# Hybrid decoder layer on one core: seven block products in place of eight in the up-projection, and a down projection of its own

## The chip, the cores and the metric

The kernel runs on one core of one Trainium2 chip. The metric is the time of one execution on the device in microseconds. Engines are named as in the profile: PE is TensorE (PEld its weight loads), DVE is VectorE, ACT is ScalarE, POOL is GpSimd, SP is SyncE, which only issues transfers.

## The reference, cut to what matters

One decoder layer, 512 positions, width 2048, everything in float32. Three groups of attention heads are mixed and projected back; then comes the feed-forward part, which the change concerns. D_FF is 5632, so `w_up` is 2048 x 11264.

```
x = x + einsum('bse,ed->bsd', mix, w_out[l])
h = rmsnorm(x, ffn_norm[l])
u = causal_dwconv(einsum('bsd,df->bsf', h, w_up[l]), conv_w[l], conv_b[l])   # three taps along the sequence
gate, up = split(u, [D_FF], axis=-1)
x = x + einsum('bsf,fd->bsd', silu(gate) * up, w_down[l])
```

## The kernel before, in words

Activations lie transposed: 16 row tiles of 128 features x 512 positions. To keep float32 accuracy at the fast rate of the float32r type, each operand is split in two float32r parts, hi (a conversion on ScalarE) and lo (the remainder, a subtraction on VectorE), and each product of a 128 x 128 weight block with a 128 x 512 activation tile is made of three matmuls, hi hi, hi lo and lo hi (`mm3`, line 262). All projections go through `product` (line 290): it takes one of two PSUM banks `pj`, accumulates over the row tiles, and spawns a task that uses the result.

Weights come in a fixed `stream` of pieces of 128 x 1024 (0.5 MB): `load_next` (line 234) issues a load into one of three buffers `wr`, `split_next` (line 241) converts half a piece at a time into buffers `wh` and `wl`, four of each, three halves ahead of their use.

The order of work is written by the program itself: the kernel is emitted in the order of a simulated clock (`Clock`, line 80) that advances with TensorE's modelled time. Small tasks are generators that yield until the clock passes their last instruction; `clock.run` resumes those that are due, `idle` moves the clock on, `drain` empties the queue. Within an engine the emitted order is the executed order; between engines semaphores are placed by the framework.

The output projection has two halves. `project_ab` (line 882) multiplies the eight tiles of groups A and B while the last heads of group C still run, and adds to the residual tiles `xn` in SBUF. Then 16 products over the tiles of group C follow, and the task `projected(m)` (line 935) scales each by the group's norm (`rg`), adds it to `xn[m]`, splits the result times the norm's gain into hi and lo (`xg2`, 32 tiles), and sums the squares on GpSimd (`sumsq`, `row_rstd`), whose result `r2` scales the rows of the up-projection afterwards.

The feed-forward part runs in chunks of eight feature tiles of the 44 (the last chunk has four). One feature tile needs two products over 16 row tiles, gate and up, so 96 matmuls of 512 columns; `conv` (line 964) applies norm, bias and taps, `gate` and `up` make silu(gate) * up and split it. The down products of one chunk, 16 of them over the chunk's tiles, are interleaved with the up-projection of the next chunk, and `summed` (line 1003) adds each to `xn[m]`.

```
        for op in ffn:
            if op[0] == "up":
                f = op[1]
                product(xg2, conv(f, f, gate))
                product(xg2, conv(NFF + f, f, up))
            else:
                c0, n = chunks[op[1]]
                product([("g", f) for f in range(c0, c0 + n)], summed(op[1], op[2]))
```

Below stand the functions that the diff touches and what calls them.

## Time and profile before

| what | value |
|---|---|
| median of 3 runs | 2230.79 us (2230.22 to 2231.01) |
| the profiled execution | 2230.37 us, its span 2228.6 us |
| TensorE busy, share of the span | 2217.2 us, 99% |
| VectorE, ScalarE, GpSimd busy | 54%, 44%, 5% |
| bytes moved | 244.26 MB, 110 GB/s in the mean |

The span runs from the first to the last instruction of the program; the execution's time has 1.8 us more around it. A busy TensorE is not TensorE at its peak, since the ends of matmuls are modelled: what a stream of them costs is read from the distance of their starts. A group of instructions is named by line, engine, operation and what it writes and reads (out<-in); line 50 is the helper through which the compute instructions are issued.

### The profile page before, as it was taken

What the parts mean: (1) busy time and instruction counts of PE and PEld (TensorE: products, weight loads), DVE (VectorE), ACT (ScalarE), POOL (GpSimd) and SP (SyncE); (2) the same over time, 40 slices, a digit from 0 to 9 for tenths busy, and PEclk for the clock granted to TensorE, in tenths of its full rate; (3) what the DMA queues carried; (4) which work ended last, traced back from release to release, by engine and by line L of the source; (5) the groups of instructions that cost most, each with busy time, mean ns of one, the idle gap of its engine ahead of it and who ended that gap; (6) DMA issues with size and microseconds to landing.
All of it is one profiled execution on the core that took longest, in us unless ns stands there. A gap on an engine that the chain in (4) does not pass through costs nothing.

```text
span 2228.6 us, 27035 instructions
## 1 busy us (share of the span) xinstructions
PE 2217.2 (99%) x10068; PEld 1838.5 (82%) x10068; DVE 1211.9 (54%) x2091; ACT 983.8 (44%) x1864; POOL 100.7 (5%) x153
## 2 busy tenths in 40 slices
PE   8999999999999999999999999999999999999999
PEld 6888888888888888888888888888888888888887
DVE  7676777767755655444444444444444444443444
ACT  6778667776754443333233333333333333232322
POOL 4000100110100200000000000000000000000000
PEclk9999999999999999999999999999999999999999
DMA  6333343334644333233333333333233333333324
GB/s 199 96 95 97 109 146 117 114 107 151 216 136 145 95 99 100 95 95 97 102 95 95 97 103 95 95 96 103 95 95 95 103 96 95 95 101 97 95 86 141
DMA packets 83082, 244.26 MB, mean 110 GB/s; under 512 B 9784, under 2 KB 13240, under 8 KB 82952
## 3 DMA queue, kind: packets, MB, share of 16 engines
q1 hardware_dynamic: 82952, 242.55, 35.0%
q8 instruction: 79, 1.29, 0.2%
q14 instruction: 51, 0.42, 0.1%
HBM read 223.05 MB, written 12.64 MB: 106 GB/s over the span
## 4 chain that ended last, share of the span: by engine, by line
PE 98%; DMA 1%; DVE 0%; issue 0%; SPq 0%; ACT 0%; DVEq 0%; ACTq 0%
PE pj L50 91%; PE s L50 5%; PE po L50 2%; PE c L50 1%; DMA wr<-in_w_in_dram 0%; DVE wl L50 0%; DMA st<-in_xT_dram 0%; SPq L128 0%; DVE sq L50 0%; DVE x L50 0%; ACT x L50 0%; DVE o L50 0%; DVE pt L50 0%; DVE sc L50 0%; ACT wh L50 0%
## 5 line engine op out<-in xcount | busy, mean ns | idle before, releaser
L50 ACT CAST wh<-wr 128x512 fp32r<-128x512 f32 (+2 forms) x782 | 476.1, 610 | 1075.4 <-PE pj L50 993.6
L50 PE MATMUL pj<-xg,wh 128*128 128x512 f32 x2816 | 867.3, 389 | 0.0
L50 DVE TENSOR_TENSOR wl<-wr,wh 128x512 fp32r<-128x512 f32 (+2 forms) x782 | 539.8, 692 | 511.5 <-ACT wh L50 503.8
L50 PE MATMUL pj<-x,wh 128*128 128x512 f32 x2272 | 710.2, 394 | 0.0
L50 PEld LDWEIGHTS pj<-xg,wh 128*128 128x128 f32 x2816 | 528.5, 188 | 110.3 <-issue 0.5
L50 PE MATMUL pj<-xg,wl 128*128 128x512 f32 x1408 | 547.7, 389 | 0.0
L50 PEld LDWEIGHTS pj<-x,wh 128*128 128x128 f32 x2272 | 415.3, 188 | 80.9 <-issue 3.0
L50 PE MATMUL pj<-x,wl 128*128 128x512 f32 x1136 | 443.7, 391 | 0.0
L50 PEld LDWEIGHTS pj<-xg,wl 128*128 128x128 f32 x1408 | 264.3, 188 | 54.8
L50 PE MATMUL pj<-mc,wh 128*128 128x512 f32 x896 | 275.7, 389 | 0.0
L50 PEld LDWEIGHTS pj<-x,wl 128*128 128x128 f32 x1136 | 213.2, 188 | 46.0
L50 PEld LDWEIGHTS pj<-mc,wh 128*128 128x128 f32 x896 | 168.2, 188 | 35.0
L50 PE MATMUL pj<-mc,wl 128*128 128x512 f32 x448 | 174.3, 389 | 0.0
L50 DVE TENSOR_TENSOR x<-pj,x 128x512 f32<-128x512 f32 x112 | 77.4, 691 | 130.3 <-PE pj L50 130.3
L50 DVE SCALAR_TENSOR_TENSOR cv<-sq,conv,cv 128x511 f32<-128x511 f32 (+1 forms) x176 | 132.2, 751 | 28.0 <-ACT cv L50 24.9
L50 DVE TENSOR_TENSOR sq<-pj,r 128x512 f32<-128x512 f32 x88 | 60.9, 692 | 138.8 <-PE pj L50 138.7
L50 PEld LDWEIGHTS pj<-mc,wl 128*128 128x128 f32 x448 | 84.1, 188 | 17.4
L50 DVE CUSTOM_DVE_ANT_0 sc<-s,strip 128x128 f32<-128x128 f32 (+3 forms) x96 | 43.7, 455 | 75.6 <-PE s L50 75.2
L50 ACT ACTIVATE cv<-sq,conv 128x512 f32<-128x512 f32 x88 | 71.9, 817 | 28.3 <-DVE sq L50 28.3
L50 ACT ACTIVATE sc<-sc,nm 128x128 f32<-128x128 f32 (+2 forms) x96 | 50.2, 526 | 1.4 <-DVE nm L50 1.3
L50 ACT CAST pt<-s 128x128 fp32r<-128x128 f32 (+2 forms) x96 | 35.7, 398 | 26.9 <-PE s L50 26.3
L50 ACT ACTIVATE sc<-sc,dn 128x128 f32<-128x128 f32 (+2 forms) x96 | 43.5, 525 | 4.3 <-DVE dn L50 4.2
(115 smaller groups left out, 1316.7 us busy)
## 6 DMA issues: line engine op xcount, KB each, us to landing
wr<-in_w_up_dram SPq DMA_DIRECT2D x176, 512.0 KB, 3.4
wr<-in_w_down_dram SPq DMA_DIRECT2D x80, 512.0 KB, 3.4
wr<-in_w_in_dram SPq DMA_DIRECT2D x78, 512.0 KB, 3.5
wr<-in_w_out_dram SPq DMA_DIRECT2D x32, 512.0 KB, 3.5
st<-st SPq DMA_DIRECT2D x48, 128.0 KB, 4.3
strip<-rb SPq DMA_DIRECT2D x24, 256.0 KB, 3.8
st<-in_xT_dram SPq DMA_DIRECT2D x16, 256.0 KB, 4.0
o_dram<-o SPq DMA_DIRECT2D x16, 256.0 KB, 4.4
```

The costliest lines, as they stand in the source:

```text
L50: res = issue(out, *args, **kwargs)
```

## The change

The up-projection is seen as a product of 2 x 2 blocks and takes seven block products instead of eight (Winograd's form of Strassen's scheme). The weights are cut into gate and up columns, and into even and odd row tiles; the activations into even and odd row tiles, and into the two halves of the sequence, 256 positions each (`HS`).

- For each pair of row tiles, `forms` makes seven blocks of 128 x 256 from the gained residual: three of the four blocks themselves and four sums, split in `TH` and `TL`, 8 tiles each, kept for the whole stage.
- For each of the 44 feature tiles (u), seven steps take a weight operand of 128 x 1024: three are blocks of `w_up` (a11, a12, a22), two are sums that the transfer makes, a plain load followed by an accumulating one issued from GpSimd (p, v), and two are sums made on VectorE (q, r). `cast` and `rest` split them three steps ahead. A step is 8 x 3 matmuls of 256 columns; four partial sums stand in halves of two PSUM banks and are copied out between steps on ScalarE. The up rows come out negated, so `nr2` is the negative of `r2`.
- `after` also does the norm, the convolution, the SiLU and the product of the tile before, and stores the result g to `g_dram`.
- Before the stage the clock is drained. The residual is kept in DRAM: `project_ab` stores it to `xab_dram`, `projected` reads it there and stores the sum to `xm_dram`.
- The down projection follows as a stage of its own: all 44 tiles g are loaded back and split (`gates`); six output tiles are accumulated chunk by chunk in six PSUM banks, the other ten one after the other over all 44 tiles. The matmuls are those of before in number and shape.

```diff
-        for op in ffn:
-            if op[0] == "up":
-                stream += [w_up[2 * t + i] for t in (op[1], NFF + op[1]) for i in range(2)]
-            else:
-                stream.append(w_down[op[1]][op[2]][:, :chunks[op[1]][1] * 128])
...
                 def task(pt):
                     vector.tensor_add(xn[m], pt, xn[m])
                     give(pt)
-                    return
-                    yield
+                    yield
+                    load(xab_dram[m], xn[m])
...
+            while "rg" not in ready or any(("mix", i) not in ready for i in MIX_ORDER[8:]):
+                idle()
+            clock.run()
+        xctx.close()
+        tctx = ctx.enter_context(ExitStack())
+        tp = tctx.enter_context(tc.tile_pool(name="tp", bufs=1, side="right", reuse_waits="tile"))
+        tr = tctx.enter_context(tc.tile_pool(name="tr", bufs=1, side="right", reuse_waits="tile"))
+        TH = [tp.tile([128, 7 * HS], F32R, name=f"th{j}") for j in range(8)]
+        TL = [tp.tile([128, 7 * HS], F32R, name=f"tl{j}") for j in range(8)]
...
+        def reload_x(m):
+            t = tr.tile([128, S], F32, name="xn", bufs=3)
+            load(t, xab_dram[m])
+            xs2.append(t)
+        def forms(j):
+            a, b = xb[2 * j], xb[2 * j + 1]
+            f = tr.tile([128, 4 * HS], F32, name="sm", bufs=2)
+            q = [f[:, i * HS:(i + 1) * HS] for i in range(4)]
+            vector.tensor_sub(q[0], a[:, :HS], a[:, HS:])
+            scalar.copy(TH[j][:, :HS], a[:, :HS])
+            vector.tensor_sub(q[1], b[:, HS:], a[:, HS:])
+            scalar.copy(TH[j][:, HS:3 * HS], b)
+            vector.scalar_tensor_tensor(q[2], b[:, HS:], -1.0, q[0], op0=ALU.mult, op1=ALU.subtract)
+            vector.scalar_tensor_tensor(q[3], q[2], -1.0, b[:, :HS], op0=ALU.mult, op1=ALU.subtract)
             yield
-            ready["mix", m] = scaled_split(t, sm[:, SM_MG + m:SM_MG + m + 1], *pair(fp, "mc", 16))
-        for i in MIX_ORDER[8:]:
-            spawn(mix_split(i))
-        spawn(group_rstd())
-        while m < KT:
-            project_ab(m)
-            m += 1
-        xg2 = [("y", m) for m in range(KT)]
-        acc = []
+            scalar.copy(TH[j][:, 3 * HS:], f)
+            vector.tensor_sub(TL[j][:, :HS], a[:, :HS], TH[j][:, :HS].bitcast(F32))
+            vector.tensor_sub(TL[j][:, HS:3 * HS], b, TH[j][:, HS:3 * HS].bitcast(F32))
+            yield
+            vector.tensor_sub(TL[j][:, 3 * HS:], f, TH[j][:, 3 * HS:].bitcast(F32))
...
+                b = tr.tile([128, S], F32, name="xb", bufs=4)
+                xb.append(b)
+                scalar.activation(b, t, AF.Copy, scale=sm[:, SM_FG + m:SM_FG + m + 1])
+                load(xm_dram[m], t)
+                if m + 3 < KT:
+                    reload_x(m + 3)
+                if m % 2:
+                    yield
+                    yield from forms(m // 2)
+                yield from sumsq(tr, acc, t, m == 0)
                 if m == KT - 1:
                     yield
-                    yield from row_rstd(fp, acc[0], D, r1)
-                    ready["r2"] = r1
-                    give(acc[0], rg[0])
+                    yield from row_rstd(tr, acc, D, r2, nr2)
...
+        STEPS = [("a11", 0, "y"), ("p", 3, "z"), ("q", 5, "y"), ("a12", 1, "x"), ("v", 4, "y"), ("r", 2, "z"),
+                 ("a22", 6, "y")]
+        raw, ops, nload = {}, {}, [0]
+        def place():
+            nload[0] += 1
+            if (nload[0] - 1) // 3 % 2 == 0:
+                return tr.tile([128, 1024], F32, name="ld", bufs=3)
+            return wp.tile([128, 1024], F32, name="wr", bufs=3)
+        def fetch(u, name):
+            if u >= NFF:
+                return
+            t = raw[u, name] = place()
+            first, second = {"a11": ((0, 0), None), "a12": ((0, 1), None), "a22": ((1, 1), None),
+                             "p": ((1, 0), (1, 1)), "v": ((0, 0), (1, 0))}[name]
+            load(t, w_up[u, first[0], first[1]])
+            if second:
+                nc.gpsimd.dma_start(t, w_up[u, second[0], second[1]], accum_op=ALU.add)
+        def add_raw(u, name, a, b):
+            if u < NFF:
+                t = raw[u, name] = tr.tile([128, 1024], F32, name="sm", bufs=2)
+                vector.tensor_add(t, raw[u, a], raw[u, b])
+        def cast(s):
+            u, j = divmod(s, 7)
+            if u < NFF:
+                hi = wq.tile([128, 1024], F32R, name="hi", bufs=4)
+                lo = wq.tile([128, 1024], F32R, name="lo", bufs=4)
+                ops[s] = hi, lo
+                scalar.copy(hi, raw[u, STEPS[j][0]])
+        def rest(s):
+            u, j = divmod(s, 7)
+            if u < NFF:
+                hi, lo = ops[s]
+                vector.tensor_sub(lo, raw[u, STEPS[j][0]], hi.bitcast(F32))
...
+        mctx.close()
+        wctx = ctx.enter_context(ExitStack())
+        wq = wctx.enter_context(tc.tile_pool(name="wq", bufs=1, reuse_waits="tile"))
+        def ahead():
+            fetch(0, "v")
+            fetch(0, "a22")
+            for x in range(3):
+                if x == 2:
+                    add_raw(0, "q", "p", "a11")
+                cast(x)
+                yield
+                rest(x)
+                yield
+        spawn(ahead())
+        clock.drain()
...
+        def after(s):
+            u, j = divmod(s, 7)
+            v = u - 1
+            if u < NFF and j == 1:
+                scalar.copy(row(u, "sg")[:, A], psy[u][:, A])
+            if u < NFF and j == 2:
+                scalar.copy(row(u, "cd")[:, B], psz[u][:, B])
+            if u < NFF and j == 3:
+                scalar.copy(post[u, "sg"][:, B], psy[u][:, A])
+            if u < NFF and j == 5:
+                scalar.copy(post[u, "cd"][:, A], psy[u][:, A])
+            cast(s + 3)
+            rest(s + 3)
+            if j == 5:
+                add_raw(u + 1, "q", "p", "a11")
+            if j == 1:
+                add_raw(u, "r", "q", "a12")
+            if u < NFF and j == 6:
+                t = row(u, "ug")
+                vector.tensor_add(t, psz[u], post[u, "sg"])
+                vector.tensor_mul(t, t, r2)
+            if v < 0:
+                return
+            if j == 0:
+                t, cd = row(v, "uu"), post[v, "cd"]
+                vector.tensor_mul(t[:, A], psy[v][:, A], nr2[:, A])
+                vector.tensor_add(t[:, B], cd[:, A], cd[:, B])
+                vector.tensor_mul(t[:, B], t[:, B], nr2[:, B])
+                scalar.activation(row(v, "cg"), post[v, "ug"], AF.Identity, bias=w(v, 3), scale=w(v, 2))
+            if j == 1:
+                scalar.activation(row(v, "cu"), post[v, "uu"], AF.Identity, bias=w(NFF + v, 3), scale=w(NFF + v, 2))
+            if j == 2:
+                taps(post[v, "cg"], post[v, "ug"], v)
+            if j == 3:
+                scalar.activation(post[v, "cg"], post[v, "cg"], AF.Silu)
+                taps(post[v, "cu"], post[v, "uu"], NFF + v)
+            if j == 4:
+                c = post[v, "cu"]
+                vector.tensor_mul(c, post[v, "cg"], c)
+                load(g_dram[v], c)
+        for s in range(7 * NFF):
+            u, j = divmod(s, 7)
+            if j == 0:
+                psy[u] = ps.tile([128, S], F32, name=f"s{u % 2}", bufs=1)
+                psz[u] = ps.tile([128, S], F32, name=f"s{2 + u % 2}", bufs=1)
+                for name in ("a11", "p", "a12"):
+                    fetch(u + 1, name)
+            if j == 3:
+                for name in ("v", "a22"):
+                    fetch(u + 1, name)
+            after(s)
+            name, form, chain = STEPS[j]
+            to = {"y": psy[u][:, A], "x": psz[u][:, A], "z": psz[u][:, B]}[chain]
+            hi, lo = ops.pop(s)
+            for k in range(8):
+                c, t = slice(k * 128, (k + 1) * 128), slice(form * HS, (form + 1) * HS)
+                tensor.matmul(to, hi[:, c], TH[k][:, t], start=j < 2 and k == 0, stop=False, skip_group_check=True)
+                tensor.matmul(to, hi[:, c], TL[k][:, t], start=False, stop=False, skip_group_check=True)
+                tensor.matmul(to, lo[:, c], TH[k][:, t], start=False, stop=k == 7, skip_group_check=True)
...
+        for j in range(5):
+            after(7 * NFF + j)
+        clock.drain()
+        wctx.close()
+        tctx.close()
+        gq = ctx.enter_context(tc.tile_pool(name="gq", bufs=1, reuse_waits="tile"))
+        GS = {f: [gq.tile([128, S], F32R, name=f"g{x}_{f}") for x in range(2)]
+              for f in [*range(36, NFF), *range(36)]}
+        def gates(f):
+            hi, lo = GS[f]
+            load(lo.bitcast(F32), g_dram[f])
+            yield
+            scalar.copy(hi, lo.bitcast(F32))
+            yield
+            vector.tensor_sub(lo, lo.bitcast(F32), hi.bitcast(F32))
+            ready["g", f] = hi, lo
...
+        wide = 6
+        stream += [w_down[c][m][:, :chunks[c][1] * 128] for c in range(len(chunks)) for m in range(wide)]
+        stream += [w_down[c][m][:, :chunks[c][1] * 128] for m in range(wide, KT) for c in range(len(chunks))]
+        for x in range(3):
+            load_next()
+        for x in range(3):
+            split_next()
...
+        for f in range(8):
+            spawn(gates(f))
+        for c, (c0, n) in enumerate(chunks):
+            for m in range(wide):
+                if c + 1 < len(chunks):
+                    for f in range(chunks[c + 1][0], sum(chunks[c + 1])):
+                        if f % 8 == m or m == 5 and f % 8 > 5:
+                            spawn(gates(f))
+                accumulate(sums[m], [("g", f) for f in range(c0, c0 + n)], range(n), None, c == 0, c == len(chunks) - 1)
                 if c == len(chunks) - 1:
-                    load(out[m], xn[m])
-                return
-                yield
-            return task
-        for op in ffn:
-            if op[0] == "up":
-                f = op[1]
-                product(xg2, conv(f, f, gate))
-                product(xg2, conv(NFF + f, f, up))
-            else:
-                c0, n = chunks[op[1]]
-                product([("g", f) for f in range(c0, c0 + n)], summed(op[1], op[2]))
+                    spawn(summed(m)(sums[m]))
+        for m in range(wide, KT):
+            pt = begin()
+            for c, (c0, n) in enumerate(chunks):
+                accumulate(pt, [("g", f) for f in range(c0, c0 + n)], range(n), None, c == 0, c == len(chunks) - 1)
+            spawn(summed(m)(pt))
```

## Rows read from the trace of the kernel before

**Rows 1.** The page's busy shares (us, share, instructions) and forty slices of the span.
```profile
span 2228.6 us, 27035 instructions
PE 2217.2 (99%) x10068; PEld 1838.5 (82%) x10068; DVE 1211.9 (54%) x2091; ACT 983.8 (44%) x1864; POOL 100.7 (5%) x153
...
PEclk9999999999999999999999999999999999999999
DMA  6333343334644333233333333333233333333324
```

**Rows 2.** The page's chain that ended last: shares of the span by engine, by line.
```profile
PE 98%; DMA 1%; DVE 0%; issue 0%; SPq 0%; ACT 0%; DVEq 0%; ACTq 0%
```

**Rows 3.** That chain in order of time, from 780 us on: start, length, what.
```profile
795.30 0.86 PE c L50 x2
796.16 1428.72 PE pj L50 x6303
```

**Rows 4.** Groups by shape on TensorE: operands, count | busy us, mean ns.
```profile
L50 PE MATMUL pj<-xg,wh 128*128 128x512 f32 x2816 | 867.3, 389 | 0.0
...
L50 PE MATMUL pj<-xg,wl 128*128 128x512 f32 x1408 | 547.7, 389 | 0.0
```

**Rows 5.** Stretches: length, busy us of each engine, granted clock, DMA share, GB/s.
```profile
core 0: us, PE busy (x) PEld busy (x) DVE busy (x) ACT busy (x) POOL busy (x), PEclk, DMA share, GB/s
6.00:9.00 3.00, 3.00 (x8) 2.32 (x7) 1.96 (x5) 2.65 (x6) 0.00 (x0) 1.00 1.02 365
...
700.60:787.40 86.80, 86.80 (x384) 71.91 (x383) 53.43 (x78) 38.75 (x62) 17.95 (x14) 1.00 0.32 97
787.60:1180.00 392.40, 392.40 (x1731) 324.53 (x1730) 188.87 (x277) 133.73 (x207) 2.33 (x2) 1.00 0.31 97
```

**Rows 6.** Timeline in attention, around 281, 360 and 425 us: start, length, engine, operation.
```profile
281.31 1.14 PEld L50 LDWEIGHTS po<-pt,av 128*128 128x128 f32 x8
...
360.52 1.11 PE L50 MATMUL po<-pt,av 128*128 128x256 f32 x8
361.47 0.63 PE L50 MATMUL s<-st,st 128*128 128x512 f32 x2
...
424.66 1.11 PE L50 MATMUL po<-pt,av 128*128 128x256 f32 x8
425.61 0.40 PE L50 MATMUL s<-st,st 128*128 128x256 f32 x2
425.85 0.82 PE L50 MATMUL s<-cst,sc 128*128 128x128 f32 x6
```

**Rows 7.** Groups by shape on VectorE, whole span.
```profile
L50 DVE TENSOR_TENSOR wl<-wr,wh 128x512 fp32r<-128x512 f32 x732 | 508.0, 695 | 500.0 <-ACT wh L50 492.3 <-PE c L50 0.4
...
L50 DVE SCALAR_TENSOR_TENSOR cv<-sq,conv,cv 128x511 f32<-128x511 f32 x88 | 66.1, 751 | 24.9 <-ACT cv L50 24.9
...
L50 DVE TENSOR_TENSOR pt<-s,pt 128x256 fp32r<-128x256 f32 x40 | 16.1, 417 | 0.5 <-ACT pt L50 0.5
```

**Rows 8.** Groups by shape on ScalarE, whole span.
```profile
L50 ACT CAST wh<-wr 128x512 fp32r<-128x512 f32 x732 | 455.0, 622 | 1033.7 <-PE pj L50 957.9 <-issue 68.9 <-PE s L50 2.8
L50 ACT ACTIVATE cv<-sq,conv 128x512 f32<-128x512 f32 x88 | 71.9, 817 | 28.3 <-DVE sq L50 28.3
...
L50 ACT CAST wh<-wr 128x256 fp32r<-128x256 f32 x34 | 13.8, 407 | 35.7 <-PE pj L50 35.7
```

**Rows 9.** The page's DMA issues: count, KB each, us from issue to landing.
```profile
wr<-in_w_up_dram SPq DMA_DIRECT2D x176, 512.0 KB, 3.4
```

**Rows 10.** Groups by shape: VectorE in the first 46 us, GpSimd over the span.
```profile
L50 DVE TENSOR_TENSOR wl<-wr,wh 128x384 fp32r<-128x384 f32 x14 | 17.0, 1253 | 0.0
...
L50 POOL TENSOR_TENSOR acc<-acc,sq 128x512 f32<-128x512 f32 x15 | 19.4, 1292 | 96.9 <-ACT sq L50 96.9
```

**Rows 11.** Timeline of TensorE from 4.5 us: first and last of its first six entries.
```profile
5.03 1.22 PE L50 MATMUL s<-x,wh 128*128 128x512 f32 x2 [5.03 <-ACT wh L50]
...
8.61 0.63 PE L50 MATMUL s<-x,wl 128*128 128x512 f32 x1
9.04 0.89 PE L50 MATMUL s<-x,wh 128*128 128x512 f32 x2
```

**Rows 12.** Timeline of the end.
```profile
2224.48 0.39 PE L50 MATMUL pj<-mc,wl 128*128 128x512 f32 x1
2224.90 0.69 DVE L50 TENSOR_TENSOR x<-pj,x 128x512 f32<-128x512 f32 x1 [2.03 <-PE pj L50]
2225.62 0.33 SPq L128 DMA_DIRECT2D out_dram<-x  x1
```

More of the change, by code (lines that the diff above doesn't have):

```diff
@@ L17 @@
 S = 512
+HS = S // 2
 D = 2048
@@ L271, in begin, with accumulate @@
             return grab(ps, "pj")
-        def accumulate(pt, acts, ks, each=None):
+        def accumulate(pt, acts, ks, each=None, first=True, last=True):
             half = min(len(acts), 8) // 2
@@ L284, in accumulate @@
                     split_next()
-                mm3(pt, hi, lo, k % half, ready[acts[k]], k == 0, k == len(acts) - 1)
+                mm3(pt, hi, lo, k % half, ready[acts[k]], first and k == 0, last and k == len(acts) - 1)
                 if each:
@@ L295, in product @@
             clock.run()
+        rows = ["sq"]
         def rstd(pool, ss, n):
-            y, a = yield from take(pool, "sq", 2)
+            y, a = yield from take(pool, rows[0], 2)
             scalar.activation(y, ss, AF.Ln, bias=epsc, scale=1.0 / n)
@@ L323, in sumsq @@
                 return
-            sq = yield from take(pool, "sq")
+            sq = yield from take(pool, rows[0])
             scalar.activation(sq, t, AF.Square)
@@ L935, in projected @@
         def projected(m):
             def task(pt):
-                t = xn[m]
-                while "rg" not in ready:
-                    yield 0.1
-                sq = yield from take(fp, "sq")
-                vector.tensor_mul(sq, pt, rg[0])
+                t = xs2[m]
+                sq = yield from take(tr, "tq")
+                vector.tensor_mul(sq, pt, rg)
                 give(pt)
@@ L962, in program @@
-        gs = {}
-        def conv(t, f, use):
-            def task(pt):
-                while "r2" not in ready:
-                    yield 0.1
-                u = yield from take(fp, "sq")
-                vector.tensor_mul(u, pt, r1)
-                give(pt)
+                    yield from row_rstd(tr, acc, D, r2, nr2)
+            return task
+        STEPS = [("a11", 0, "y"), ("p", 3, "z"), ("q", 5, "y"), ("a12", 1, "x"), ("v", 4, "y"), ("r", 2, "z"),
+                 ("a22", 6, "y")]
@@ new lines, in rest @@
+        def rest(s):
[4 more added lines that the diff above has]
+        for name in ("a11", "p", "a12"):
+            fetch(0, name)
+        for i in range(3):
+            reload_x(i)
+        for i in range(KT):
+            product([("mix", x) for x in MIX_ORDER[8:]], projected(i))
+        mctx.close()
+        wctx = ctx.enter_context(ExitStack())
+        wq = wctx.enter_context(tc.tile_pool(name="wq", bufs=1, reuse_waits="tile"))
@@ new lines, in w, with taps @@
+        def w(t, i):
+            return cv[:, 4 * t + i:4 * t + i + 1]
+        def taps(c, x, t):
+            vector.scalar_tensor_tensor(c[:, 1:], x[:, :S - 1], w(t, 1), c[:, 1:], op0=ALU.mult, op1=ALU.add)
+            vector.scalar_tensor_tensor(c[:, 2:], x[:, :S - 2], w(t, 0), c[:, 2:], op0=ALU.mult, op1=ALU.add)
+        psy, psz = {}, {}
+        A, B = slice(0, HS), slice(HS, S)
+        def after(s):
[38 more added lines that the diff above has]
+                load(g_dram[v], c)
@@ new lines, in program @@
+        for s in range(7 * NFF):
[3 more added lines that the diff above has]
+                psz[u] = ps.tile([128, S], F32, name=f"s{2 + u % 2}", bufs=1)
+                for name in ("a11", "p", "a12"):
+                    fetch(u + 1, name)
[11 more added lines that the diff above has]
+                tensor.matmul(to, lo[:, c], TH[k][:, t], start=False, stop=k == 7, skip_group_check=True)
+            clock.run()
@@ L971, in task, with summed @@
+        wide = 6
[5 more added lines that the diff above has]
+            split_next()
+        def summed(m):
+            def task(pt):
+                t = gq.tile([128, S], F32, name="xo", bufs=3)
+                load(t, xm_dram[m])
                 yield
-                c = yield from take(fp, "cv")
@@ L1003, in summed @@
[L1003 to L1020 removed]
+                load(out[m], t)
@@ L1021, in program @@
+        for m in range(wide, KT):
[3 more added lines that the diff above has]
+            spawn(summed(m)(pt))
+            clock.run()
         clock.drain()
```

101 lines of the change are left out of this document (42 added, 59 removed).

## The prediction

> **What bounds the kernel now.** I read the busy shares first: TensorE is busy 99% of the span at a granted clock of 9 in every slice, the other engines half of it or less, the transfers a third [rows 1]. The chain of waits that ended last says the same: TensorE 98%, 91% of it the products of the projections [rows 2]. So the time is the number of products times their spacing, plus whatever stops TensorE. In order of time, the last link of that chain is one run of 6303 products in 1428.72 us, 0.2267 us each, without a gap; before it stand two sum-of-squares products of 0.86 us [rows 3]. The up-projection owns 2816 + 1408 = 4224 products of 512 columns [rows 4], so 957.6 us. With the 44 x 16 x 3 = 2112 of the down projection the feed-forward part is 6336 products, and counted back from 2224.88 it starts at about 787.6 us. The stretches by engine show the room beside it: from 787.6 to 1180 us VectorE is busy 189 of 392 us and ScalarE 134; in the second half of the output projection (700.6 to 787.4) VectorE 53 and ScalarE 39 of 87 [rows 5].
>
> **The products.** The new up-projection has 44 groups x 7 steps x 8 row tiles x 3 = 7392 products, of 256 columns. Columns fall from 44 x 96 x 512 to 44 x 168 x 256, by one eighth; but a product costs more than its columns: 512 columns at 2.4 GHz are 0.2133 us and the trace pays 0.2267. No projection here has 256 columns, but attention does: eight such products, each with a weight load of its own, start at 360.52 and the next one at 361.47; ten start at 424.66 and the next at 425.85: 0.119 us each [rows 6]. That is 12 ns over the columns' 0.107. Then the up-projection takes 7392 x 0.119 = 879.6 us, a gain of 78.0. Every nanosecond in this spacing is 7.4 us. Such runs are short, and a weight load that keeps up for ten products may not for thousands, so I keep 0.117 to 0.123 for the range (-14.8 to +29.6).
>
> The Trainium skill (TensorE: Matmul & The Clock Gate, section Back-to-back issue gap) puts a product at N / 2.4 + 2.5 ns, 109 ns for 256 columns and 216 for 512. By it the gain would be 911 - 807 = 104 us, an estimate from that page. The rows have 119 and 227, so the sum goes by them.
>
> **What VectorE, ScalarE and transfers do beside it.** A group lasts 168 x 0.119 = 20.0 us. VectorE's prices: 0.695 us for 512 columns of two operands, 0.417 for 256, 0.751 for a tap of the convolution [rows 7]; 1024 columns, which the trace doesn't have, are 0.695 + 2 x 0.278 = 1.25. A group has seven remainders and two block sums of 1024 (11.3 us), three operations of 512 (2.1), three of 256 (1.25), four taps (3.0): 17.6 us, 88%. By step it is 1.9 to 2.75 us against 2.86. The operands are made three steps ahead, so a late one has some 4 us before TensorE misses it. I cost this at nothing, but the cover is thin: once VectorE needs over 20 us a group, the excess is paid 44 times. ScalarE: seven conversions of 1024 at 1.05 (0.622 plus two times the step from 0.407 [rows 8]), four copies of 256, two scalings of 0.817, a SiLU of about 0.63: 11.2 us. The copies out of PSUM stand in front of conversions in its queue, and each waits only for the step just ended.
>
> Transfers: per group five loads of 0.52 MB, two accumulating ones, a store of 0.26: 3.93 MB in 20 us, 197 GB/s. At the start the kernel moved 365 GB/s with the engines full [rows 5], so there is room. The accumulating transfer isn't in the trace. A plain load of this size lands in 3.4 us [rows 9]; GpSimd must first wait for the first half, and behind it in GpSimd's queue stands only the next such transfer. Issue to first use is five steps, 14.3 us, and TensorE needs the result three steps later. From below it costs nothing; it binds when two of them take over 20 us, three times the load's time each. I take nothing, being nearest to the load.
>
> **The second half of the output projection.** Per product VectorE gets 2 x 0.692 for the residual, half of a set of forms (four of 256, remainders of 256, 512 and 1024: 4.0 / 2 = 2.0) and 1.4 for two weight remainders: 4.8 of 5.44 us, where before there were 3.5. GpSimd adds squares for 1.29 us in each product, and where its additions stood beside VectorE's (first 46 us) a 384-column remainder took 1.253 instead of the 0.55 between 256 and 512 [rows 10]. With one such loss of 0.7 a product it comes to 5.5: level. I take +1 us, with 0 to 5. The extra stores and reloads of x stay hidden, at a DMA share of 0.32 there [rows 5].
>
> **The seam before the up-projection.** Today products of the up-projection run on while the last row's squares are summed. Now the whole queue is drained first: the sum-of-squares product stands ahead of all up products in TensorE's order. From the last product on: multiply and add on VectorE 1.4, scaling on ScalarE 0.7, a weight remainder of 1024 ahead of the forms 1.25, four forms 1.7, conversion of 1024 columns 1.05, square 0.63, GpSimd's addition 1.29 [rows 10], the product 0.86 [rows 3]: 8.9, with handovers 9.0, of which 0.86 were there before: +8.1. Without the forms it would be 5, with all of `ahead` in front 16.
>
> **The seam before the down projection.** After the last step VectorE has 1.25 for u, 1.5 and 1.5 for the taps, 0.7 for the gate; then SyncE stores g, 5.0 us on. The weight loads of the down projection are issued behind that store, and the reload of the first g behind three of them: 1.83 MB at 365 GB/s are 5.0, plus the 2.0 of a 3.4 us load that aren't its 1.4 of bytes: 7.0. Conversion and remainder 1.3. Sum +13.3, with 8 (g and weights land early) and 20.
>
> **The clock.** After idling from the start TensorE ran its first nine products from 5.03 to 9.04, 0.45 apart [rows 11], near the 0.427 of 512 columns at 1.2 GHz, though the granted clock of 6 to 9 us reads 1.00 [rows 5]; against 0.2267 that lost 2.0 us. Nothing in this trace shows how a gap of 9 or 13 us is answered; I take 2.0 for each seam, with 0 as the other bound. The tail is unchanged: last product 2224.48, addition, store [rows 3, 12].
>
> **The sum.** The profiled execution took 2230.37 us (its span 2228.6 and 1.8 around it), 0.4 under the median of the three. 2230.4 - 78.0 + 1.0 + 8.1 + 2.0 + 13.3 + 2.0 = 2178.8, so 2179 us, -2.3%.
>
> **The rivals.**
> *The weight load sets the pace.* Half as many columns per load leave the load nothing to hide under: eight loads of such a run take 1.14 us, about as long as the products [rows 6]. If a steady stream runs at 0.130, the up-projection takes 961 us and the kernel 2260: slower. It decides from 0.1260 on. Against it: 0.119 holds over ten.
> *VectorE becomes the bound.* If it loses 0.7 us [rows 10] to GpSimd on five operations in a group, a group takes 21.1 us: +48, 2227; with more, 2240.
> *Accumulating transfers are slow.* At 12 us each, 24 us a group: +176, 2355. They turn the gain into a loss above 10.6 us each. For it: nothing measured; against it: the free bandwidth.
> *No fixed cost per product.* If a 256-column product costs half of a 512-column one, 0.1133, the gain is 120 us and the time 2137. The rows of 0.119 speak against it. The Trainium skill (TensorE: Matmul & The Clock Gate, Back-to-back issue gap) goes further still, to 0.109.
>
> **How the numbers follow.** Forecast 0.66, weight load 0.09, VectorE 0.11, transfers 0.09, no fixed cost 0.05. The forecast's own range, from its bounds, is 2150 to 2226. To hold 8 in 10 the range takes in VectorE and the near half of the weight-load case and leaves out slow transfers and the cheap product: 2148 to 2248. The runs before lie within 0.8 us; 0.2% (4.5 us) is about what a measurement can tell from no change. Faster: the forecast, the cheap product and a third of the VectorE case, 0.75. Slower: 0.20. Within 0.2%: 0.05.
>
> **What would show it.** Right: products of the up-projection 0.119 apart; two idle stretches of TensorE, 9 and 13 us, and none of over a microsecond between; VectorE near 88% in the up stage. Wrong: TensorE waiting once a group for a remainder (VectorE) or for a conversion behind an accumulating load (transfers), or products evenly spaced at over 0.126 with no wait (weight load).

## The result, and the profile after

The changed kernel takes 2207.7 us in the median (2206.9 to 2209.1), beside 2230.6 for the kernel before: a ratio of 0.990 (95% interval 0.988 to 0.992). It is faster, inside the range, but by 23 us where 52 were forecast. The profiled execution took 2207.63 us. Of all executions below, one of the six of e19_best64 took 2166.0 us where the other five took 2133.4 to 2134.8; it is left out of that version's ratio. The page's span, busy shares and slices, then the chain that ended last by engine:

```profile
span 2205.8 us, 34567 instructions
...
PE 2163.0 (98%) x13236; PEld 1935.8 (88%) x13236; DVE 1453.4 (66%) x2229; ACT 1148.5 (52%) x2020; POOL 181.5 (8%) x241
...
PEclk9999999999999989999999999999999899999999
DMA  6322343334657557777777777777773554433332
...
PE 94%; DMA 3%; DVE 1%; issue 1%; ACT 0%; SPq 0%; POOL 0%; DVEq 0%; POOLq 0%; ACTq 0%
```

TensorE still sets the time, but the chain, 98% TensorE in [rows 2], now has 6% of other things, and two slices are below 9 in the clock: the two seams. The stretches by engine show them beside the up-projection (length, busy us of each engine, granted clock, DMA share, GB/s):

```profile
core 0: us, PE busy (x) PEld busy (x) DVE busy (x) ACT busy (x) POOL busy (x), PEclk, DMA share, GB/s
...
709.20:802.00 92.80, 88.48 (x385) 71.48 (x383) 64.23 (x106) 45.32 (x78) 18.48 (x13) 1.00 0.54 171
802.00:818.00 16.00, 1.36 (x3) 0.84 (x3) 14.43 (x17) 7.42 (x11) 6.43 (x4) 0.55 0.70 197
818.00:1706.40 888.40, 888.40 (x7393) 887.89 (x7391) 715.74 (x829) 469.11 (x615) 75.84 (x87) 1.00 0.72 191
1706.40:1720.00 13.60, 0.27 (x4) 0.07 (x2) 6.68 (x12) 3.90 (x7) 0.00 (x0) 0.69 0.56 202
```

And the chain in order of time (start, length, what): 51 products of the first stage, the whole up-projection as one piece, the reload of g at the second seam:

```profile
46.11 11.89 PE pj L51 x51
...
818.71 887.95 PE s L51 x7392
1713.44 5.76 DMA g<-g_dram
```

7392 products in 887.95 us are 0.1201 each, without a gap. But the 51 products of the first piece are 0.2331 apart, where the same 51 products before were

```profile
45.78 11.60 PE pj L50 x51
```

0.2275 each. So a stage that the change does not touch became slower, too. Stage by stage, from the starts of TensorE's products:

| stage | forecast, us | measured, us | off by |
|---|---|---|---|
| start to second half of output projection (700.6 before) | 700.6 | 709.2 | +8.6 |
| second half of output projection | 86.8 + 1.0 | 90.8 | +3.0 |
| seam before the up-projection | 9.0 | 17.75 | +8.7 |
| up-projection with its cold start | 879.6 + 2.0 | 888.8 | +7.2 |
| seam before the down projection | 13.3 | 13.5 | +0.2 |
| down projection with its cold start | 478.7 + 2.0 | 481.9 | +1.2 |

The sum of the last column, 28.9, is the distance from 2178.8 to 2207.6. What VectorE, ScalarE and the accumulating transfers cost in the up stage is as forecast: nothing. The 1.25 and 1.05 us worked out from [rows 7] and [rows 8] are 1.23 and 1.05, and a plain load lands in 4.5 us instead of the 3.4 of [rows 9]. Groups by shape (busy, mean ns) and the page's DMA issues (count, KB, us to landing):

```profile
L51 DVE TENSOR_TENSOR lo<-ld,hi 128x1024 fp32r<-128x1024 f32 x111 | 137.0, 1234 | 28.9 <-ACT hi L51 28.9
...
L51 ACT CAST hi<-ld 128x1024 fp32r<-128x1024 f32 x111 | 116.5, 1050 | 21.7 <-PE s L51 21.7
...
ld<-in_w_up_dram SPq DMA_DIRECT2D x111, 512.0 KB, 4.5
...
ld<-in_w_up_dram POOLq DMA_DIRECT2D x45, 512.0 KB, 5.6
```

### The profile page after: what moved, and what is told of

Its sections match the earlier page's. It is cut to its first block, busy times and chain, and to the rows that moved or that the text cites. A ratio compares the mean times of both kernels' runs of the same rounds, so it can differ in the third digit from the quotient of the medians.

```text
span 2205.8 us, 34567 instructions
## 1 busy us (share of the span) xinstructions
PE 2163.0 (98%) x13236; PEld 1935.8 (88%) x13236; DVE 1453.4 (66%) x2229; ACT 1148.5 (52%) x2020; POOL 181.5 (8%) x241
## 4 chain that ended last, share of the span: by engine, by line
PE 94%; DMA 3%; DVE 1%; issue 1%; ACT 0%; SPq 0%; POOL 0%; DVEq 0%; POOLq 0%; ACTq 0%
PE s L51 50%; PE pj L51 39%; PE po L51 3%; PE c L51 2%; DMA xm_dram<-xn 1%; DMA wr<-in_w_out_dram 1%; DVE wl L51 0%; DVE tl L51 0%; DMA xn<-xab_dram 0%; DMA wr<-in_w_in_dram 0%; SPq L129 0%; DMA g<-g_dram 0%; DMA wr<-in_w_up_dram 0%; DMA st<-in_xT_dram 0%; POOL gacc L51 0%
## 5 line engine op out<-in xcount | busy, mean ns | idle before, releaser
L51 PE MATMUL s<-th,hi 128*128 128x256 f32 x2464 | 698.6, 284 | 0.0
L51 PE MATMUL s<-tl,hi 128*128 128x256 f32 x2464 | 697.7, 283 | 0.0
L51 PE MATMUL s<-th,lo 128*128 128x256 f32 x2464 | 697.7, 283 | 0.0
L51 DVE TENSOR_TENSOR wl<-wr,wh 128x512 fp32r<-128x512 f32 (+2 forms) x430 | 298.0, 698 | 342.2 <-ACT wh L51 340.5
L51 ACT CAST wh<-wr 128x512 fp32r<-128x512 f32 (+2 forms) x430 | 256.3, 598 | 486.4 <-PE pj L51 310.0
L51 PE MATMUL pj<-x,wh 128*128 128x512 f32 x1504 | 479.2, 400 | 0.0
L51 PEld LDWEIGHTS s<-th,hi 128*128 128x128 f32 x2464 | 473.6, 192 | 0.5 <-issue 0.5
L51 PEld LDWEIGHTS s<-tl,hi 128*128 128x128 f32 x2464 | 473.6, 192 | 0.5 <-issue 0.5
L51 PEld LDWEIGHTS s<-th,lo 128*128 128x128 f32 x2464 | 473.5, 192 | 0.0
L51 PE MATMUL pj<-g,wh 128*128 128x512 f32 x880 | 271.0, 389 | 0.0
L51 DVE TENSOR_TENSOR lo<-ld,hi 128x1024 fp32r<-128x1024 f32 x111 | 137.0, 1234 | 28.9 <-ACT hi L51 28.9
L51 PE MATMUL s<-g,wh 128*128 128x512 f32 x352 | 110.7, 396 | 13.5 <-ACT g L51 13.3
```

Of the source, the lines that this page charges most:

```text
L51: res = issue(out, *args, **kwargs)
```

## The experiments

### The stage that was not touched: where the operands lie

The change moves the x tiles to the right side of SBUF, where they begin 480 bytes past a multiple of 512; the weights' buffers begin on a multiple. (The tile `end`, 480 bytes, puts TH and TL back on one.) Theory: products whose moving operand is off a multiple of 64 bytes are slower. Rival: the extra stores slow the first 700 us. **e1_align** puts x on a multiple of 512.

```diff
+        vector.memset(xp.tile([128, 120], F32, name="top"), 0.0)
         xctx.close()
```

> The changed kernel with one 480-byte tile above the x tiles, so that each of the 32 tiles starts on a multiple of 512 bytes instead of 32 bytes beside one; they stay on the right side. If the offset makes the 512-column products slower (0.2325 us apart in the changed kernel, 0.227 before), the projections of the first 700 us come back to 0.227, the second half of the output projection starts at 700.6 us instead of 709.2, and the kernel takes 2199 us. If the side itself or the rest of the changed program does it, the spacing stays at 0.2325 and the time at 2207.7.

2198.6 us, ratio 0.986 (0.984 to 0.987); the second half of the output projection begins at 701.3 us instead of 709.2. The stores are all still there, so the rival fell. **e2_off** does the opposite to the kernel before: 32 bytes ahead of x.

```diff
+        off = xp.tile([128, 8], F32, name="off")
...
+        vector.memset(off, 0.0)
```

> The kernel before with a 32-byte tile ahead of the x tiles, and nothing else. If the offset of 32 bytes costs the products their 5 ns, the projections of the first 700 us go from 0.227 to 0.2325 us and the kernel from 2230.6 to some 2239 us; the attention tiles behind x are moved by 32 bytes too. If the side did it, nothing changes: 2230.6.

2284.3 us, ratio 1.024: far more than expected, since the pools behind x (all operands of the feed-forward part) move with it. The chain's one long piece, [rows 3] before, says what a product pays:

```profile
808.28 1470.70 PE pj L50 x6303
```

0.2333 instead of 0.2267. **e13_off64** and **e15_off128** have 64 and 128 bytes instead of 32; **e12_th32** and **e16_th64** make `end` of the changed kernel 128 and 136 floats long instead of 120, which moves TH and TL by 32 and 64 bytes. Their pool fills the right side of SBUF from its top, so a longer `end` moves them down: they begin 480 and 448 bytes past a multiple of 512, not 32 and 64, which the expectations of these two runs overlook. (e13_off64 and e15_off128 to e18_w32 are one execution each, and so is e11_head further down; a spacing is still the mean over 6303 or 7392 products.)

```diff
-        vector.memset(tp.tile([128, 120], F32, name="end"), 0.0)
+        vector.memset(tp.tile([128, 128], F32, name="end"), 0.0)      # e12_th32
```

> The kernel before with a tile of 64 bytes in front of x, where 32 bytes cost 53 us (0.2333 us a product instead of 0.2267). If what matters is that the moving operand begins at a multiple of 64 bytes, the products are 0.2267 apart and the time is that of before, 2230.6 us. Rival: it is any shift against a larger unit (128 bytes or more, or the place of one tile against another): 0.2333 and 2284 us.

> The changed kernel with the tile `end` 32 bytes longer, so that all tiles TH and TL, the moving operands of the up-projection, begin 32 bytes past a multiple of 64. If a 32-byte offset costs each product the 6.7 ns that 512 columns paid, 7392 products lose 49 us and are 0.127 apart: 2257 us. If it is paid by the column, 3.3 ns, 0.1235 apart: 2232 us. If 256 columns pay nothing, 0.120 apart and 2208 us. I expect the middle one, 2232.

2247.9 us at 64 bytes, so a multiple of 64 isn't enough, and 2194.3 us (ratio 0.984) with TH and TL moved by 32: faster, 13 us under the change. The long pieces of e13_off64 (0.2289 a product) and of e12_th32 (0.1184 with the cold start):

```profile
799.62 1442.70 PE pj L50 x6303
```

```profile
818.23 875.54 PE s L51 x7392
```

My theory of alignment fell twice. What is left is that the place of the moving operand counts by itself (A) or against the weights that are being loaded (B). **e17_both32** puts the 32 bytes ahead of weights and activations, **e18_w32** ahead of the weights, with activations moved by 512.

```diff
+        off = cp.tile([128, 8], F32, name="off")          # e17_both32 and e18_w32
+        off2 = xp.tile([128, 120], F32, name="off2")      # e18_w32 alone
...
```

> The kernel before with 32 bytes put ahead of everything (a tile in the pool of constants), so that the weights' buffers and the activations are moved by the same 32 bytes. Theory A, the place of the moving operand in SBUF counts: 0.2333 a product, 2284 us as with x alone moved. Theory B, its place against the weights that are loaded meanwhile counts: 0.2267 and 2230.6 us.

> The kernel before with the weights' buffers moved by 32 bytes and the activations by 512. Theory A (the moving operand's own place counts): 0.2267 and 2230.6 us. Theory B (its place against the weights counts): 0.2333 or near it, 2284 us; with 480 bytes between the two instead of 32 it may be as far off the other way, 0.229 to 0.2333.

2230.9 and 2284.2 us. With both moved nothing is lost; with the weights alone moved the activations' own place is as good as before and the loss is there in full. The same long piece of the chain, of e17_both32:

```profile
796.68 1428.72 PE pj L50 x6303
```

and of e18_w32:

```profile
807.97 1470.70 PE pj L50 x6303
```

Theory B stands: what counts is the place of the moving operand against the weights. The two remaining offsets:

> The changed kernel with TH and TL moved by 64 bytes. For 512 columns 0, 32 and 64 bytes gave 0.2267, 0.2333 and 0.2289; for 256 columns 0 and 32 gave 0.1200 and 0.1183. If the order of the offsets is the same in some sense at 256 columns, 64 lies between, 0.119 (2200 us). If every offset off 512 is as good as 32: 0.1183 and 2194. If the offset against the weights' 512-byte blocks opens a hole that grows with the offset: below 0.1175, 2188 or less.

> The kernel before with a tile of 128 bytes ahead of x; 0, 32, 64 bytes of offset against the weights gave 0.2267, 0.2333 and 0.2289 at 512 columns. If the loss has its peak at 32 and dies away: 0.2267 to 0.228, 2231 to 2241 us. If, as at 256 columns with 64 bytes, there is an offset at which the products come closer than at 0: 0.220 to 0.224, 2180 to 2210 us. I expect the first.

2155.7 us with TH and TL moved by 64 bytes, its up-projection

```profile
817.11 838.70 PE s L51 x7392
```

0.1135 a product with the cold start, 0.1133 without; and 2281.9 us with x at 128 bytes, where I had expected no loss:

```profile
805.69 1470.71 PE pj L50 x6303
```

All together, spacing in us by the offset of the moving operand against the weights' 512-byte blocks (at 480, 512 columns are e18_w32 and 256 columns e12_th32; 448 is e16_th64):

| offset, bytes | 0 | 32 | 64 | 128 | 448 | 480 |
|---|---|---|---|---|---|---|
| 512 columns | 0.2267 | 0.2333 | 0.2289 | 0.2333 | not run | 0.2333 |
| 256 columns | 0.1200 | not run | not run | not run | 0.1133 | 0.1183 |

The row of 512 columns neither falls nor rises evenly. Only 0 and 480 were run with both widths: at 480 the products of 512 columns lose 6.6 ns and those of 256 gain 1.7, so an offset that is good for one width need not be for the other. How the memory makes this is not shown, nor that the loading of weights at the same moment is what collides.

### The seam before the up-projection

In the last 16 us before the up stage VectorE is busy 14.4 (the stretch 802 to 818 above). The timeline there (start, length, engine, operation, idle before and its releaser):

```profile
799.75 0.39 PE L51 MATMUL pj<-mc,wl 128*128 128x512 f32 x1
...
803.49 0.68 DVE L51 TENSOR_TENSOR tq<-pj,r 128x512 f32<-128x512 f32 x1
...
807.08 1.22 DVE L51 TENSOR_TENSOR lo<-ld,hi 128x1024 fp32r<-128x1024 f32 x1
...
809.80 1.04 ACT L51 CAST th<-sm 128x1024 fp32r<-128x1024 f32 x1 [1.25 <-DVE sm L51]
810.00 0.88 POOL L1007 DMA_DIRECT2D wr<-in_w_up_dram  x1 [11.31 <-DVE sm L51]
810.60 5.98 POOL L51 TENSOR_TENSOR gacc<-gacc,tq 128x512 f32<-128x512 f32 x3
810.62 2.65 DVE L51 TENSOR_TENSOR lo<-ld,hi 128x1024 fp32r<-128x1024 f32 x1
812.21 0.63 ACT L51 ACTIVATE tq<-xn 128x512 f32<-128x512 f32 x1 [1.36 <-POOL gacc L51]
813.19 2.28 DVE L51 TENSOR_TENSOR tl<-sm,th 128x1024 fp32r<-128x1024 f32 x1
...
816.64 2.07 PE L51 MATMUL c<-gacc,cst 128*128 128x512 f32 x2 [16.50 <-POOL gacc L51]
```

GpSimd's last three additions start only at 810.60, behind an accumulating transfer in its queue that had waited 11.3 us. Theory: that transfer (v of the first tile) holds the squares up. **e3_late** issues it and the load of a22 after the drain.

```diff
         def ahead():
-            fetch(0, "v")
-            fetch(0, "a22")
...
         clock.drain()
+        fetch(0, "v")
+        fetch(0, "a22")
```

> The changed kernel with the first v and a22 fetched only after the clock is drained, so that no accumulating transfer stands ahead of the last additions of squares in GpSimd's queue. If that transfer, which waits for its plain half, holds up the additions, TensorE's wait before the up-projection falls from 17.8 us to 9 or 10, and the kernel takes 2199 to 2200 us. If VectorE's backlog of forms and remainders alone sets the wait, it stays above 15 us and the kernel above 2205.

2207.4 us: no change, the seam 18.5. The last addition now waits for the last square, at 813.28 on ScalarE, behind a conversion that itself waits for VectorE. So it is the queue of ScalarE and VectorE's backlog. The backlog has a source: in the second half VectorE waits for the reload of x (waits of VectorE, 709 to 802 us: total, times, longest), and SyncE, which issues it, for squares and stores (waits of SyncE, 700 to 802 us):

```profile
DVE xn L51 <- DMA xn<-xab_dram: 15.7, 10, 3.0
```

```profile
SPq L129 <- DMA xm_dram<-xn: 48.6, 12, 5.3
SPq L129 <- ACT tq L51: 14.7, 5, 8.7
```

The reload of row m + 3 takes the buffer of row m, whose last readers are the store and the square. **e5_reload** issues reloads one product later (row m + 2), when they are free; **e6_square** puts the square ahead of the forms; **e7_square_late** is the second with e3_late.

```diff
-                if m + 3 < KT:
-                    reload_x(m + 3)
+                if 0 < m < KT - 2:            # e5_reload
+                    reload_x(m + 2)
...
+                yield from sumsq(tr, acc, t, m == 0)      # e6_square
                 if m % 2:
                     yield
                     yield from forms(m // 2)
-                yield from sumsq(tr, acc, t, m == 0)
```

> The changed kernel with each reload of the residual issued one product later, when the store that frees its buffer has landed. If SyncE, waiting for that store, delays the weights of the output projection behind it (SyncE waits 48.6 us for such stores between 700 and 802 us), the second half of the output projection falls from 90.6 us to 87 or 88 and the kernel to 2204 or 2205. If VectorE's load makes TensorE wait there, nothing changes: 90.6 and 2207.7.

> The changed kernel with each row's square issued ahead of its forms instead of behind them. Now I hold that two things bound the wait before the up-projection to nearly the same length: the last square stands in ScalarE's queue behind the forms and behind a conversion that waits for VectorE, and GpSimd's last additions stand behind the accumulating transfer. Then this one alone leaves the second: the wait stays at 15 to 18 us and the kernel at 2205 to 2208. If the place of the square is the whole cause, the wait falls to 9 or 10 us and the kernel to 2199 or 2200.

> The same, and the first v and a22 fetched after the drain as well. If the two causes stand one behind the other, the wait before the up-projection falls from 17.8 us to 9 or 10, and the kernel to 2199 or 2200. If VectorE's backlog itself sets the wait (forms, remainders), it stays above 14 us.

| | second half | seam | up-projection | time, us | ratio |
|---|---|---|---|---|---|
| the change | 90.8 | 17.75 | 888.8 | 2207.7 | 0.990 (0.988 to 0.992) |
| e5_reload | 87.05 | 12.35 | 889.3 | 2198.6 | 0.986 (0.984 to 0.987) |
| e6_square | 87.05 | 6.9 | 892.9 | 2197.2 | 0.985 (0.984 to 0.986) |
| e7_square_late | 87.05 | 6.5 | 895.9 | 2199.6 | 0.986 (0.985 to 0.988) |

e5_reload takes VectorE's waits for x from 15.7 us to 0.4 and gains 9.1 us, three times what I expected, since the backlog behind the seam goes with them. The place of the square by itself is enough for the seam, so that my division into two causes fell. e6_square also brings the second half to the same 87.05 us without moving a reload: VectorE's waits for x are gone, SyncE's waits for squares fall from 14.7 to 0.9 us, and those for the stores stay (51.1 us). So of the two last readers it was the square, standing behind the forms, that held the buffer; the two edits cure one cause. TensorE's named waits in the second half, 2.4 us in the change, are for VectorE and ScalarE; in both runs there are none.

The early transfer in GpSimd's queue costs nothing that matters; issued late it costs the up stage 3 us once the seam is short. And a short seam is paid for in part: 17.75 us had let VectorE work ahead, now the first groups wait, 1.4 us in e6_square, and TensorE has 33 intervals of over 0.15 us, where the change has ten (892.9 against 888.8 us). Of the 33, 27 lie in the first 7.5 us of the stage, most of them 0.213 apart at a granted clock of 0.50; in the change this clock ends 2.9 us into the stage.

### The seam before the down projection

**e4_front** issues the first three loads of w_down two steps before the end of the up stage, lets the first g be loaded into room that is free by then, and stores the last g behind the loads of the first eight.

```diff
+            if s == 7 * NFF - 2:
+                for x in range(3):
+                    load_next()
...
-              for f in [*range(36, NFF), *range(36)]}
+              for f in range(NFF)}
...
-                load(g_dram[v], c)
+                if v < NFF - 1:
+                    load(g_dram[v], c)
...
+        clock.run()
+        load(g_dram[NFF - 1], post[NFF - 1, "cu"])
```

> The changed kernel with the first three weight pieces of the down projection loaded during the last steps of the up-projection, the first eight g tiles in the place of the up-projection's weight operands (free with its last product), and the store of the last g behind their loads. If the order in SyncE's queue (store, weights, g) sets the wait before the down projection, it falls from 13.5 us to about 7 and the kernel to 2201. If VectorE's tail and the conversions set it, it stays above 11 us and the kernel above 2205.

2202.7 us, ratio 0.987 (0.986 to 0.989): the seam falls from 13.5 to 5.7, and 1.9 us come back as small waits for g in the down projection (483.8 against 481.9).

### How far the other engines stood from the bound

**e11_head** leaves out the products hi x TL from the second tile on.

```diff
+                if u == 0:
                     tensor.matmul(to, hi[:, c], TL[k][:, t], start=False, stop=False, skip_group_check=True)
```

> The changed kernel without the products hi x TL from the second feature tile on, so that a group has 112 products of 256 columns instead of 168; everything on VectorE, ScalarE, GpSimd and the transfers is left as it is. (Part of the computation is left out: a third of the up-projection's products.) It asks how far the other engines stood from setting the pace. If TensorE still set it, a group would take 112 x 0.120 = 13.4 us. VectorE was busy 16.3 us a group, which with handovers makes 16.5 to 17.5 us: an up stage of 725 to 770 us, a total of 2045 to 2090, and TensorE waiting for remainders. Rival, the transfers set the pace: at two accumulating ones of 5.6 us and three plain ones of 4.5 in flight nothing would show below 16.3; if they serialise, a group takes 18 us or more (795 us, 2115) and the waits end with a load in GpSimd's or SyncE's queue.

2144.3 us; the up stage takes 822.1, that is 18.6 us a group. It is more than the 725 to 770 that I expected. What TensorE waits for, and what stands behind it (waits, 1000 to 1400 us; `wh` is here a partial sum that ScalarE copies out of PSUM):

```profile
ACT hi L51 <- DVE sm L51: 105.3, 42, 3.8
...
PE s L51 <- ACT wh L51: 65.9, 22, 3.5
DVE lo L51 <- ACT hi L51: 50.7, 43, 1.2
```

VectorE is busy 347 of these 400 us: the sums q and r go from VectorE to ScalarE and back, each waits for the other, and TensorE waits for a copy that stands behind them in ScalarE's queue. The accumulating transfers still land in 5.6 us and SyncE waits for a DMA for under 1 us in the stretch. GpSimd does wait for the plain halves, as in the change, but the chain that ended last holds no transfer there (1000 to 1400 us, shares by line):

```profile
by line: DVE lo L51 31.1%; PE s L51 18.3%; issue 14.0%; DVE sm L51 10.0%; ACT hi L51 9.2%; DVE wl L51 9.1%; DVE wh L51 7.4%; ACT wh L51 0.7%; ACTq L51 0.3%; DVEq L51 0.2%
```

So the number is near that of the transfers' rival, the waits are not. The other engines let a group of 18.6 us pass, 8% under the 20.16 of the change. Part of the 18.6 is TensorE's own: with a stop in each group its granted clock is 0.88 in this stretch. How far they would go at full clock was not run.

### All of it together

**e9_all** has e1_align, e3_late, e4_front, e5_reload and the square ahead; **e10_best** the same without e3_late; **e14_best32** and **e19_best64** are e10_best with TH and TL moved by 32 and 64 bytes, to 480 and 448.

> All edits that the theories call for in one kernel: x tiles on a multiple of 512 bytes (9 us, measured), the order before the down projection (5 us, measured), the later reload (3 us), the square ahead of the forms and the later first fetch (8 us). If the parts add up, 2207.7 - 25 = 2183 us; if the last two fail, 2194.

> The changed kernel with the tile that aligns x, the reload of x on even terms, the square ahead of the forms, and the front of the down projection, but with the fetches of v and a22 where the change has them (inside `ahead`). The run that held all five edits took 2184.9 us and its up-projection ran from 793.75 to 1688.3, 894.6 us, where the changed kernel's takes 888.8. Theory: the late fetch is what the up stage paid there, so this run has an up stage of 888 to 890 us; its seam is 6.9 us as in the run with the square alone, not 6.2, and its time 2180 us (2178 to 2183). Rival: the first groups wait because TensorE starts cold and VectorE is behind after a short seam, whatever the fetch: the up stage stays at 894 and the time at 2185 or more.

> The version with aligned x, reload, square and front of the down projection (2182.3 us), with all tiles TH and TL moved by 32 bytes as well, which by itself made the products of the up-projection 0.1183 apart instead of 0.1200. If that is a property of the operand's place, it comes on top: 7392 x 1.67 ns = 12.3 us, 2170 us (2168 to 2173). Rival: the 2194.3 us of that run came from elsewhere (its second half of the output projection began as late as the change's, so little is left for this): 2178 or more.

> The version of 2182.3 us with TH and TL moved by 64 bytes instead of 32. Alone this brought the products of the up-projection from 0.1200 to 0.1133 apart. On top of the other edits, from the 2169.8 us at 0.1183: 7392 x 5.0 ns = 37 us, 2133 us (2130 to 2138). A group then lasts 19.04 us, and with a third of the products left out VectorE and its handovers to ScalarE needed 18.7 us. Rival: after the short seam TensorE catches VectorE up while it is still behind, there are only 0.3 us a group to recover, and the waits go on for many groups: 2140 or more.

| | seam 1 | up-projection | seam 2 | time, us | ratio |
|---|---|---|---|---|---|
| e9_all | 5.95 | 894.7 | 5.7 | 2184.9 | 0.980 (0.978 to 0.981) |
| e10_best | 5.8 | 892.7 | 5.7 | 2182.3 | 0.978 (0.977 to 0.980) |
| e14_best32 | 6.0 | 880.4 | 5.7 | 2169.8 | 0.973 (0.971 to 0.974) |
| e19_best64 | 6.4 | 843.3 | 5.7 | 2134.5 | 0.957 (0.956 to 0.958) |

The late fetch explains 2 of the 6 us that the up stage of e9_all is over the change's; the other 4 are the short seam's. In e19_best64 TensorE doesn't stop from 850 us on, with VectorE at 641 of 750 us, 86%:

```profile
850.00:1600.00 750.00, 750.00 (x6620) 750.00 (x6619) 641.43 (x748) 416.67 (x550) 68.55 (x79) 1.00 0.77 208
```

Its group of 19.04 us (168 x 0.1133) is just over the 18.6 of e11_head. By these two numbers some 2 ns a product (0.4 us / 168) are left before VectorE and ScalarE would set the pace, an estimate.

## Why the prediction was right and wrong

Of the 28.9 us between forecast and result, 8.6 are products that the change does not touch, 7.2 the size of the new products' spacing, 8.7 the first seam and 3.0 the second half of the output projection.

**Right.** The up-projection goes at an even spacing with no wait of TensorE in 44 groups, at 0.1200 where 0.119 was read from ten products; the nanosecond is 7.4 us and inside the stated 0.117 to 0.123. That these rows of attention told so well was luck: their operands `pt` and `av` both begin 96 bytes past a multiple of 512, so they stand at offset 0 to each other as the new ones do, which the prediction did not look at. VectorE has 715.7 / 44 = 16.3 us a group where 17.6 were counted. Accumulating transfers land in 5.6 us, half of the 10.6 at which they would have decided. The second seam is 13.5 for 13.3, and its parts agree: 5.1 us until the store of the last g is issued (5.0), 7.6 until the first g has landed (7.0), 0.8 for its conversion (1.3, with the remainder). Both cold starts are there: nine of the first ten intervals of the up stage are 0.213, what 256 columns are at 1.2 GHz, with a granted clock of 0.55 in the stretch before; of the 2.0 taken for it 1.7 are measured, half of it in the first interval, in which the second sum-of-squares product still runs. At the second seam most of the first dozen products are 0.427 apart, 2.7 us lost where 2.0 were taken. These gaps do lower the clock, which no row of before showed.

**Wrong, the term that was missing.** The sum has no term for what the change leaves alone: it takes 0.2267 for a property of 512 columns. It is one of the operand's place: the first 700 us became 8.6 us longer, and putting x back on a multiple of 512 gave back 7.9 of them (e1_align). The same holds for the new products. 0.1200 is the spacing at offset 0; 0.1133, the price of the rival "no fixed cost per product", is that at offset 448 (e16_th64), and the weight load, a rival at 0.130, keeps up there. The Trainium skill (SBUF — State Buffer, section A bandwidth-pool intuition that's wrong (but worth ruling out)) gives weight loads a second, independent read port beside the moving operand's; the runs don't fit full independence, since 32 bytes between the two make 0.2333 of 0.2267 and nothing changes when both move. The 109 ns that the Trainium skill's formula makes for 256 columns (TensorE: Matmul & The Clock Gate, section Back-to-back issue gap, which gives it for a single product) no run reached: 113.3 is the closest.

**Wrong, the first seam.** The step "with handovers 9.0" priced the last row's work as if VectorE were level when the last product ends. It was a whole product behind: the last row's multiplication is at 803.49, 3.7 us after the last product, and the remainders of 1024 columns that run beside GpSimd's additions last 2.3 to 2.65 us, those without 1.22. That backlog came from the reloads is shown by e5_reload, where the seam falls to 12.35; with the square ahead of the forms it is 6.9 (e6_square), under the 9.0. The upper bound of 16, "with all of `ahead` in front", is near what happened, for another reason.

**Wrong, stores and reloads.** "The extra stores and reloads of x stay hidden" rested on a DMA share of 0.32. It is a matter of order, not of bytes: the reload stands on SyncE behind the release of its buffer, and VectorE waited 15.7 us for it. That is 4.0 us in the second half where +1 was taken (3.75 come back in e5_reload), and about 5 of the seam. "Behind it in GpSimd's queue stands only the next such transfer" was false as well at the seam, but cost nothing (e3_late).

## What to carry to other kernels

A spacing of matmuls read from a trace belongs to the addresses of that kernel: whoever moves a pool should measure the products that read it, and try a few offsets of the moving operand against the weights, one line each (here from -2.4% to +2.4% of the whole kernel). Where a buffer is reloaded, look for its last reader in that engine's queue; where a stage is drained, count what the engines are behind, not only the last row's work.

## What was not expected of the hardware

The spacing of float32r products depends on the offset between the moving operand and the weight blocks in SBUF: 0.2267 to 0.2333 us at 512 columns, 0.1133 to 0.1200 at 256, over the offsets that were run. An accumulating transfer of 512 KB lands in 5.6 us beside 4.5 for a plain one.
